# Hybrid decoder step (RG-LRU and mLSTM): other numbers of main matmuls between the side steps

## The chip, the cores and the metric

The kernel runs on one core of one Trainium2 chip. The metric is the device time of one execution in microseconds. Before the change the median of three timed runs is 949.22 us (947.42 to 950.13).

## The reference

One layer of a hybrid decoder step, on a prompt of 1024 positions (zero state) and on one new token for each of 8 sequences that already have a state. Both groups of heads read the same normalised input:

```
hn = rmsnorm(x, g_norm)
u = hn @ w_in                       # 1024 -> 7176
xa, za, q, k, v, o, zb, ui, uf = split(u)
yA = rglru(xa)                      # conv of 4 taps, two gates of 16 blocks 64x64, scan
yB = mlstm(q, k, v, ui, uf)         # 4 heads, DK = DV = 256, chunks of 128
yB = rmsnorm_head(sigmoid(o) * yB)
x = x + concat(yA * silu(za), yB * silu(zb)) @ w_out
y = rmsnorm(x, g_final)
```

RG-LRU: with `r`, `i` sigmoids of the block gates, `a = exp(-8 r softplus(-lam))`, and `h = a * h + sqrt(1 - a^2) * i * xc` is a scan over the positions. mLSTM carries a matrix `C` (256 x 256 for a head), a vector `n` and a running maximum `m`; one chunk uses the scores `q k^T` of its 128 positions with a decay mask, and the state for what lies before it. The outputs are both `y`, and for prompt and tokens the last `h`, the last three inputs of the conv, `C`, `n` and `m`. Everything is float32.

## The kernel before

**Main matmuls.** A float32 product is made of three fp32r matmuls: each operand is split into a high part (a cast on ScalarE, L70) and a low part (a subtraction on VectorE, L71), and `mm3` (L62 to L66) issues high x high, high x low and low x high. The input projection is cut into 14 units of two blocks of 256 columns, in the order `UNITS = v0v1 x0y0 q0k0 x1y1 q1k1 x2y2 v2v3 q2k2 x3y3 q3k3 o0o1 o2o3 z0z1 z2z3` (x is xa, y is za). A unit is computed by seven products of sums of blocks (`Q_P1` to `Q_P7`); `prep` builds the operand of one of them, two products ahead. `product(u, q)` runs one product in two halves and yields after each. The prediction calls one matmul of L64 to L66 a main.

**Side work.** Unit 0 runs at the start. For the other 13 units, after each half of a product, `pop_bg` takes steps from three queues: `bg` (two steps in unit 1 and in the last unit, else one), `rgq` (one), and `dcq` (one, at every second half of a product for units under 10, at every third from then on). A step issues a few instructions and so takes a place between main matmuls.

- `bg` holds first the generator `gates()`, one step a call (L563 to L666): the parameter rows are loaded and transposed (L588, PE), decays and exponentials are computed (L596 to L617), the rows of forget and input gates are transposed (L627, PE, into banks `ps_s` and `ps_qp`) and scanned (L632, L633, VectorE), four stacks of rows `stk` are written (L651 to L654), five empty steps follow (L655), and the stacks are transposed (L661, PE, one half of the chunks to `ps_s`, one to `ps_qp`). `rd_open` stands behind them: it opens the buffers of the gate weights and of the decode step.
- `rgq` holds the steps of RG-LRU for a block j of 128 channels and a half b of the positions, `rg_half`: `conv1`, `conv2`, `lows`, `gate_a` and `gate_b` (L786, PE: `ps_s<-xh` and `ps_tr<-xl`), `decay`, `scan`, `outs`. The prediction calls one such pair (j, b) a chunk of RG-LRU.
- `dcq` holds the decode steps of a head (`decode_steps`): `first`, then one `token(b)` for each of the 8 tokens. A token's state `Cb` is loaded on SyncE (L911), scaled on ScalarE (L932), updated on VectorE with the broadcast `vbc` (L905, L934), multiplied with q on PE (L953) and stored on GpSimd (L936).
- `dec_unit` computes the tokens' part of a unit's projection (L236) when its fifth product is prepared, and its turn (L244, a transpose, and L247, a reduction on VectorE) is run at one of the next pops. L236 and L244 use the PSUM bank `ps_tr`, as `gate_b` does. L261 and L262 build the operand of that product in place.

**The last unit and mLSTM.** When q, k and v of all heads are there and the queues are empty, `m_start` opens the mLSTM buffers and adds `m_first(n)` for the heads' first chunks: scores (L1126, L1128 on PE into `ps_s`), then the product with the state (`ps_qp<-Ch,qh`). In the last unit `wo_prep` loads the rows of the output projection (`oraw`, L1248 on SyncE), multiplies them with the tokens' merged values (L1270, PE, into `ps_tr`) and splits them (L1279, L1280, L71). Then the loop over the mLSTM chunks follows, with the output projection as its main matmuls.

**Order.** The program is written in the order of the loops, and a scheduler places each engine's instructions in a fixed queue by that order and by when it believes their operands to be ready. Each engine runs its queue in order. SyncE (SP) issues loads, GpSimd (POOL) issues stores; of the PSUM tiles, `ps_o` has three buffers, `ps_kv` two, and `ps_s`, `ps_qp` and `ps_tr` one each, which the prediction calls banks.

Of the kernel before, what the change touches and what calls it, by code (L numbers as in the profile page):

```python
# [20 lines left out]
NB = 8  # L21
# [28 lines left out]
def hymba_kernel(  # L50
# [17 lines left out]
    def split(hi, lo, src):  # L68

        A.copy(hi, src)  # L70
        V.tensor_tensor(lo, src, hi.bitcast(F32), op=ALU.subtract)  # L71
# [7 lines left out]
    def ps(tag, shape):  # L79
        return psp.tile(shape, F32, tag=tag, name=f"ps_{tag}", bufs=NBUF.get(tag, 1))  # L80
# [425 lines left out]
    kind, j = units[0][0]  # L506
# [61 lines left out]
    def gates():  # L568
# [48 lines left out]
        A.activation(dEM, dm, AF.Exp, scale=-1.0)  # L617
        stq(s_m, dm[0:1])
        yield

        rows = fp.tile([NH, 2, T], F32, tag="rows0", name="rows0")
        lfr, igr = rows[:, 0, :], rows[:, 1, :]
# [29 lines left out]
        A.copy(stk[32:36], br)  # L652
        V.tensor_tensor(c3(stk[64:68]), c3(br), aL.unsqueeze(2).to_broadcast([NH, NCH, L]), op=ALU.add)
        A.mul(stk[96:100], mr, -1.0)  # L654
        for _ in range(5):  # L655
            yield
        for half in range(2):
            pk = ps(("s", "qp")[half], [P, 4, P])
# [14 lines left out]
    bg, rgq, dcq = deque(), deque(), deque()  # L673
# [64 lines left out]
    def rg_gw(j):  # L738
        if j < KC:
            graw = fpr["graw"][j % 2]  # L740
            for n, src in enumerate((w_rgate, w_igate)):
                for s in LOHI:
                    ld(graw[s, :, n * 64:n * 64 + 64], src[0, 2 * j:2 * j + 2].rearrange("t c d -> c t d"))

    def rg_half(j, b):
        fp = fpr["p"]
        pc = lambda r, n=1: PT[:, j, r:r + n]
        st = {}

        n = 2 * j + b  # L750

        def conv1():
            rg_load(n, True)
            xs = st["xs"] = rst["x", n]
            rg_load(n + 1)
            if b == 0:
                rg_gw(j + 1)
                ghi = fp.tile([P, 2, P], F32R, tag="ghi", name="ghi")
                glo = fp.tile([P, 2, P], F32R, tag="glo", name="glo")
                split(ghi, glo, fpr["graw"][j % 2])  # L760
                rst["g", j] = ghi, glo
            st["xc"] = xc = fp.tile([P, HT], F32, tag="xc", name="xc")
            V.tensor_scalar(xc, xs[:, 3:3 + HT], pc(R_CW + 3), pc(R_CB), op0=ALU.mult, op1=ALU.add)
            for t in (2, 1):
                V.scalar_tensor_tensor(xc, xs[:, t:t + HT], pc(R_CW + t), xc, op0=ALU.mult, op1=ALU.add)

        def conv2():
            xs, xc = st["xs"], st["xc"]
            V.scalar_tensor_tensor(xc, xs[:, 0:HT], pc(R_CW), xc, op0=ALU.mult, op1=ALU.add)
            st["xx"] = [fp.tile([P, HT], F32R, tag=t, name=t) for t in ("xh", "xl")]  # L770
            for n, s in enumerate(LOHI):
                x = st["xx"][n]
                A.copy(x[s], xc[s])
            if b == 1:
                V.tensor_copy(OC[:, j, 1:4], xs[:, HT:HT + 3])

        def lows():
            for n, s in enumerate(LOHI):
                x = st["xx"][n]
                V.tensor_tensor(x[LOHI[1 - n]], st["xc"][s], x[s].bitcast(F32), op=ALU.subtract)  # L780

        def gate(n):

            pg = ps(("s", "tr")[n], [P, 512])
            for k, w in enumerate(rst["g", j]):
                TE.matmul(pg, w[:, n, :], st["xx"][n], start=k == 0, stop=k == 1)  # L786
            return pg

        def gate_a():
            rg_load(n + 1, True)  # L790
            pg = gate(0)
            st["rg"], st["ig"] = (fp.tile([P, HT], F32, tag=t, name=m) for m, t in (("rg", "rg"), ("ig", "xh")))
            gate_out(st["rg"], st["ig"], pg, j, 0)

        def gate_b():
            pg = gate(1)
            gate_out(st["rg"], st["ig"], pg, j, 1)
            st["na"] = fp.tile([P, HT], F32, tag="xl", name="na")
            A.activation(st["na"], st["rg"], AF.Tanh, scale=sp2[:, j:j + 1], bias=sp2[:, j:j + 1])
            A.activation(st["rg"], st["rg"], AF.Exp, scale=sp4n[:, j:j + 1], bias=sp4n[:, j:j + 1])  # L800
            V.scalar_tensor_tensor(st["ig"], st["ig"], 1.0, st["xc"], op0=ALU.add, op1=ALU.mult)

        def decay():
            rg, na = st["rg"], st["na"]
            V.scalar_tensor_tensor(na, rg, 1.0, na, op0=ALU.add, op1=ALU.mult)
            V.tensor_scalar(rg, na, -1.0, 1.0, op0=ALU.mult, op1=ALU.add)
            V.scalar_tensor_tensor(na, na, 2.0, na, op0=ALU.subtract, op1=ALU.mult)
            A.activation(na, na, AF.Sqrt, scale=-0.25)

        def scan():  # L810
            rg, ig, na = st["rg"], st["ig"], st["na"]
            V.tensor_tensor(ig, ig, na, op=ALU.mult)
            V.tensor_tensor_scan(na, rg, ig, 0.0 if b == 0 else OC[:, j, 0:1], op0=ALU.mult, op1=ALU.add)
            V.tensor_copy(OC[:, j, 0:1], na[:, HT - 1:HT])

        def outs():
            na, zs = st["na"], rst["z", n]
            V.scalar_tensor_tensor(na, na, 0.5, zs, op0=ALU.mult, op1=ALU.mult)
            mh, ml = sg([P, HT], "rmh", F32R), sg([P, HT], "rml", F32R)
            split(mh, ml, na)  # L820
            stq(d_rm[0, j, :, b * HT:(b + 1) * HT], mh.bitcast(F32))
            stq(d_rm[1, j, :, b * HT:(b + 1) * HT], ml.bitcast(F32))
        return [conv1, conv2, lows, gate_a, gate_b, decay, scan, outs]

    def rg_dec(j):

# [86 lines left out]
    def decode_steps(h):  # L913

        p2 = fpr["p"]
        qsel, qfirst, selq = fpr["qsel"], fpr["qfirst"], fpr["selq"]
        st = {}

        def first():
            st["kw"] = kw = p2.tile([P, 2, NB], F32, tag="kw", name="kw")  # L920
            V.tensor_tensor(kw, dk[:, 2 * h:2 * h + 2, :], dW[:, :, h].unsqueeze(1).to_broadcast([P, 2, NB]), op=ALU.mult)
            V.tensor_copy(qsel.rearrange("p k (m r) -> p k m r", r=9)[:, :, :, 0:5:4],
                          dq[:, 2 * h:2 * h + 2, :].rearrange("p k (m r) -> p k m r", r=2))
            V.tensor_copy(qfirst[:, :, :, 0], dq[:, 2 * h:2 * h + 2, 0:2])
            fetch_v(h, 0)

        def token(b):
            i = h * NB + b

            def f():  # L930
                vb_, C = ds_.pop(("v", i)), ds_["C", i]
                A.mul(C, C, dGI[:, b, h:h + 1])  # L932
                for kb in range(2):
                    V.scalar_tensor_tensor(C[:, kb, :], vb_, st["kw"][:, kb, b:b + 1], C[:, kb, :],  # L934
                                           op0=ALU.mult, op1=ALU.add)
                stq(s_C[0, b, h].rearrange("(kb p) v -> p kb v", p=P), C)  # L936
                if b + 1 < NB:
                    fetch_v(h, b + 1)
                if b % 2:
                    late.append(lambda: late.append(products))  # L940
                else:
                    fetch_C(i + 2)
                    fetch_C(i + 3)


            def products():
                if b == 1:
                    st["pq"] = ps("qp", [P, 512])
                pq = st["pq"]
                for g in range(4):  # L950
                    bb, kb = b - 1 + g // 2, g % 2
                    q, n = (qfirst[:, kb, bb, :], 32) if b == 1 else (qsel[:, kb, 4 * bb:4 * bb + 4], 4)
                    TE.matmul(pq[32 * g:32 * g + n, 0:256], q, ds_["C", h * NB + bb][:, kb, :], start=b == 1,  # L953
                              stop=b == NB - 1, skip_group_check=True)
                for bb in (b - 1, b):
                    del ds_["C", h * NB + bb]
                if b == NB - 1:
                    Z = sg([P, 256], "qC")
                    V.tensor_copy(Z, pq[:, 0:256])

                    def turn():
                        pt = pq[:, 256:272].rearrange("p (v b) -> p v b", v=2)
                        for vb in range(2):
                            TE.matmul(pt[:, vb, :], Z[:, vb * P:(vb + 1) * P], selq, start=True, stop=True)
                        V.tensor_copy(dqC[:, 2 * h:2 * h + 2, :], pt)
                    late.append(lambda: late.append(turn))
            return f
        return [first] + [token(b) for b in range(NB)]


    def bh(t):
# [454 lines left out]
    def preps(n):  # L1426
        while state["prep"] < min(n, len(seq)):
            prep(*seq[state["prep"]])
            state["prep"] += 1

    gg = gates()
    bg.extend([lambda: next(gg, None)] * 17 + [rd_open])
    last_u = len(units) - 1
    unit_of = {p: u for u, pair in enumerate(units) for p in pair}
    done_h = [max(unit_of[k, h] for k in "qkv") for h in range(NH)]
# [56 lines left out]
    for n in range(4, N):  # L1492
        c, h = n // 4, n % 4
# [84 lines left out]
```

## Time and profile before

| | before |
|---|---|
| timed runs, median (lowest to highest) | 949.22 us (947.42 to 950.13) |
| the profiled execution | 944.93 us |
| its span | 943.1 us |
| TensorE busy | 921.4 us |
| VectorE, ScalarE, GpSimd busy | 711.7, 587.2, 145.7 us |
| HBM read, written | 100.59, 51.65 MB |

The profile is one execution, with its own time. A row of a timeline gives the start in us, the length of the instruction (or of a run of like ones, with their count), the engine (PE is TensorE, DVE VectorE, ACT ScalarE, POOL GpSimd, SP SyncE), the line, the operation, what it writes and reads, its shape, and in brackets the idle time of the engine just before it with what ended it. Matmuls overlap, so the distance between two starts, and not the length, says what one costs. A row of waits gives what waited for what, with the sum, the count and the longest in us.

### The profile page before, as it was taken

How to read it: one execution, taken by the hardware profiler on the slowest of the kernel's cores; microseconds unless marked ns; L12 is line 12 of the kernel's file. 1: busy time of each engine (PE TensorE's matmuls, PEld its weight loads, DVE VectorE, ACT ScalarE, POOL GpSimd, SP SyncE). 2: the span in 40 equal slices, each digit the busy share in tenths (PEclk: the TensorE clock that was granted, in tenths of full speed). 3: DMA queues.
4: the chain of work that ended last, by engine and by line, in shares of the span. 5: the costliest groups of instructions: out<-in, count | busy, mean ns of one | idle time of the engine just before them, and what ended most of it. 6: DMA issues, size and time to landing. Idle time of an engine off the chain costs nothing. (4 is left out here: it accounts for less than half of the span.)

```text
span 943.1 us, 15351 instructions
## 1 busy us (share of the span) xinstructions
PE 921.4 (98%) x5350; PEld 761.0 (81%) x5350; DVE 711.7 (75%) x1465; ACT 587.2 (62%) x1052; POOL 145.7 (15%) x259
## 2 busy tenths in 40 slices
PE   9999999999999999999999999999899999999997
PEld 7797767777787987787789898876578888888886
DVE  6784898889798878888797867687657676676764
ACT  7563457778677757677578774467537466555532
POOL 1111112112112122111122221010201000000020
PEclk9999999999999999999999999999999999999999
DMA  5521347356746464545557362426953564464461
GB/s 174 187 82 45 134 132 276 107 181 203 243 145 207 157 207 165 176 140 189 193 180 248 131 209 87 157 88 229 343 159 111 162 187 122 142 187 140 122 103 46
DMA packets 131384, 153.19 MB, mean 162 GB/s; under 512 B 15817, under 2 KB 110057, under 8 KB 131299
## 3 DMA queue, kind: packets, MB, share of 16 engines
q1 hardware_dynamic: 113578, 96.34, 34.0%
q0 software_dynamic: 17728, 55.87, 16.5%
q8 instruction: 42, 0.69, 0.3%
q14 instruction: 36, 0.29, 0.1%
HBM read 100.59 MB, written 51.65 MB: 161 GB/s over the span
## 5 line engine op out<-in xcount | busy, mean ns | idle before, releaser
L71 DVE TENSOR_TENSOR wl<-raw,wh 128x1024 fp32r<-128x1024 f32 x91 | 110.9, 1219 | 27.2 <-ACT wh L70 17.2
L70 ACT CAST wh<-raw 128x1024 fp32r<-128x1024 f32 x91 | 95.4, 1048 | 54.9 <-PE ps_o L65 23.3
L64 PE MATMUL ps_kv<-cb_hi,wh 128*128 128x512 f32 x320 | 127.8, 399 | 0.6 <-ACT s L319 0.6
L66 PE MATMUL ps_kv<-cb_hi,wl 128*128 128x512 f32 x320 | 125.3, 392 | 0.0
L65 PE MATMUL ps_kv<-cb_lo,wh 128*128 128x512 f32 x320 | 125.2, 391 | 0.0
L64 PE MATMUL ps_o<-cb_hi,wh 128*128 128x512 f32 x240 | 95.1, 396 | 0.0
L66 PE MATMUL ps_o<-cb_hi,wl 128*128 128x512 f32 x240 | 94.0, 392 | 0.0
L65 PE MATMUL ps_o<-cb_lo,wh 128*128 128x512 f32 x240 | 93.6, 390 | 0.0
L64 PEld LDWEIGHTS ps_kv<-cb_hi,wh 128*128 128x128 f32 x320 | 60.1, 188 | 22.1 <-issue 4.2
L66 PEld LDWEIGHTS ps_kv<-cb_hi,wl 128*128 128x128 f32 x320 | 60.1, 188 | 13.9 <-issue 0.8
L65 PEld LDWEIGHTS ps_kv<-cb_lo,wh 128*128 128x128 f32 x320 | 60.2, 188 | 12.6 <-issue 0.8
L64 PE MATMUL ps_kv<-wh,cb_hi 128*128 128x256 f32 x192 | 55.4, 288 | 0.0
L64 PEld LDWEIGHTS ps_o<-cb_hi,wh 128*128 128x128 f32 x240 | 45.1, 188 | 11.5 <-issue 2.5
L65 PE MATMUL ps_kv<-wl,cb_hi 128*128 128x256 f32 x192 | 54.3, 283 | 0.0
L66 PE MATMUL ps_kv<-wh,cb_lo 128*128 128x256 f32 x192 | 54.3, 283 | 0.0
L64 PE MATMUL ps_o<-wo,rh 128*128 128x512 f32 (+1 forms) x136 | 53.8, 396 | 0.0
L65 PEld LDWEIGHTS ps_o<-cb_lo,wh 128*128 128x128 f32 x240 | 45.1, 188 | 10.0 <-issue 0.8
L66 PEld LDWEIGHTS ps_o<-cb_hi,wl 128*128 128x128 f32 x240 | 45.1, 188 | 9.8
L66 PE MATMUL ps_o<-wo,ml 128*128 128x512 f32 (+1 forms) x136 | 52.1, 383 | 0.7 <-DVE ml L71 0.7
L64 PE MATMUL ps_o<-wo,mh 128*128 128x512 f32 (+1 forms) x136 | 52.8, 388 | 0.0
L66 PE MATMUL ps_o<-wo,rl 128*128 128x512 f32 (+1 forms) x136 | 51.8, 381 | 0.3 <-DMA rl<-d_rm 0.3
L65 PE MATMUL ps_o<-wo,rh 128*128 128x512 f32 (+1 forms) x136 | 51.6, 379 | 0.0
(481 smaller groups left out, 2530.2 us busy)
## 6 DMA issues: line engine op xcount, KB each, us to landing
raw<-in_w_in_dram SPq DMA_DIRECT2D x55, 512.0 KB
Cb<-in_state_mlstm_C_dram SPq DMA_DIRECT2D x32, 256.0 KB
out_dram<-Cb POOLq DMA_DIRECT2D x32, 256.0 KB, 4.6
qk<-d_qk SPq DMA_DIRECT2D x32, 256.0 KB
oraw<-in_w_out_dram SPq DMA_DIRECT2D x16, 512.0 KB
d_qk<-s POOLq DMA_DIRECT2D x24, 256.0 KB, 3.9
d_x<-s POOLq DMA_DIRECT2D x16, 256.0 KB, 2.6
zsr<-d_y SPq DMA_DIRECT2D x16, 256.0 KB
```

Of the source, the lines that this page charges most:

```text
L64: TE.matmul(out, ah, bh, start=first, stop=False, skip_group_check=True)
L65: TE.matmul(out, ah, bl, start=False, stop=False, skip_group_check=True)
L66: TE.matmul(out, al, bh, start=False, stop=last, skip_group_check=True)
L70: A.copy(hi, src)
L71: V.tensor_tensor(lo, src, hi.bitcast(F32), op=ALU.subtract)
```

## The change

Five edits, all of them empty steps: in the generator of the gates one more yield ahead of the transposes of the rows, and seven empty steps for five ahead of the transposes of the stacks; the queue calls the generator 18 times for 17; for the first halves (b = 0) of the blocks j = 0 and 1, RG-LRU's queue has an empty step ahead of `gate_a`; head 0's decode has one between `first` and the first token.

```diff
@@ -617,6 +617,7 @@
         A.activation(dEM, dm, AF.Exp, scale=-1.0)
         stq(s_m, dm[0:1])
         yield
+        yield
 
         rows = fp.tile([NH, 2, T], F32, tag="rows0", name="rows0")
...
@@ -652,7 +653,7 @@
         V.tensor_tensor(c3(stk[64:68]), c3(br), aL.unsqueeze(2).to_broadcast([NH, NCH, L]), op=ALU.add)
         A.mul(stk[96:100], mr, -1.0)
-        for _ in range(5):
+        for _ in range(7):
             yield
         for half in range(2):
             pk = ps(("s", "qp")[half], [P, 4, P])
...
@@ -820,7 +821,8 @@
             stq(d_rm[1, j, :, b * HT:(b + 1) * HT], ml.bitcast(F32))
-        return [conv1, conv2, lows, gate_a, gate_b, decay, scan, outs]
+        wait = [lambda: None] if j < 2 and b == 0 else []
+        return [conv1, conv2, lows] + wait + [gate_a, gate_b, decay, scan, outs]
@@ -965,7 +967,7 @@
             return f
-        return [first] + [token(b) for b in range(NB)]
+        return [first] + [lambda: None] * (h == 0) + [token(b) for b in range(NB)]
@@ -1429,7 +1431,7 @@
     gg = gates()
-    bg.extend([lambda: next(gg, None)] * 17 + [rd_open])
+    bg.extend([lambda: next(gg, None)] * 18 + [rd_open])
```

## The prediction

> **What bounds the kernel now.** I read the busy shares and the chain of waits first, then TensorE's waits, then the stretches around the largest ones.
>
> ```profile
> span 943.1 us, 15351 instructions
> PE 921.4 (98%) x5350; PEld 761.0 (81%) x5350; DVE 711.7 (75%) x1465; ACT 587.2 (62%) x1052; POOL 145.7 (15%) x259
> PE 18%; DVE 3%; DMA 2%; issue 1%; ACT 0%; SPq 0%; DVEq 0%; ACTq 0%
> PE ps_tr L1270 <- DMA oraw<-in_w_out_dram: 2.8, 3, 2.0
> PE ps_s L661 <- DVE stk L653: 1.7, 1, 1.7
> PE ps_s L786 <- DVE xh L780: 1.6, 2, 1.3
> PE ps_kv L64 <- ACT s L319: 0.6, 1, 0.6
> PE ps_s L627 <- DVE gx L599: 0.3, 1, 0.3
> ```
>
> TensorE (PE) is busy for 921.4 of 943.1 us, and it leads the chain. A change of order can win only what PE loses in waits, about 22 us in all, plus clock. The waits are in us: total, times, longest. The steps of the gates that the change moves are L627, L661 and L786; their waits add up to 0.3 + 1.7 + 1.6 us. The largest single wait stands elsewhere, at the start of the mLSTM stage, and it has a price beyond itself:
>
> ```profile
> 120.00:140.00 20.00, 18.32 (x90) 14.58 (x87) 19.85 (x38) 8.65 (x19) 3.64 (x9) 1.00 0.48 139
> 680.01 1.93 PE L1270 MATMUL ps_tr<-oraw,mBd 128*32 128x512 f32 x8 [2.01 <-DMA oraw<-in_w_out_dram]
> 680.00:682.00 2.00, 1.99 (x9) 0.33 (x9) 0.77 (x1) 1.15 (x1) 0.59 (x2) 0.50 1.17 305
> 682.00:684.00 2.00, 2.00 (x8) 1.81 (x9) 0.88 (x3) 1.09 (x3) 0.55 (x1) 0.65 1.19 299
> 684.00:686.00 2.00, 2.00 (x11) 1.62 (x10) 0.59 (x2) 0.26 (x1) 0.00 (x0) 1.00 1.07 339
> ```
>
> The columns of the windows: length, busy PE, weight loads, DVE, ACT, POOL, granted clock, DMA share, GB/s. After the 2.01 us gap the clock is 0.50 in one window and 0.65 in the next. That loses 2 x 0.50 + 2 x 0.35 = 1.70 us, so the gap costs 3.7 us. The gap of 1.7 us at L661 lies in the first of these windows, whose clock is 1.00.
>
> **The change part by part.** The built instruction lists of the two kernels hold the same instructions; only their order differs. I call the wide products of L64 to L66 "mains"; one takes 0.23 us (140.72 to 140.95 below). Positions are counted in mains ahead of an instruction:
>
> ```
> gates rows, L627 (ps_qp)        +12 and +4
> gates, L588, L627 (ps_s), L661  no change
> first gate product, chunk (0,0) no change (629)
> chunk (0,1) ps_s, ps_tr         +12, +17 (720 -> 737)
> chunk (1,0) ps_s                +23 (805 -> 828)
> later chunks                    +18 to +49
> first decode product, L953      +36 (828 -> 864)
> first score products, L1126     +48 (2688 -> 2736)
> score products of chunk 4       -24 (3096 -> 3072)
> from main 3168 on (709 us)      no difference
> ```
>
> *The gates (an extra yield, 7 for 5 empty ones, 18 generator steps).* Their waits stand at L661 and L786:
>
> ```profile
> 125.15 1.22 DVE L653 TENSOR_TENSOR stk<-rows,gsm 4x1024 f32<-4x1024 f32 x1
> 126.51 0.63 PE L661 MATMUL ps_s<-idF,stk 128*128 128x128 f32 x4 [1.68 <-DVE stk L653]
> 141.31 0.89 DVE L934 SCALAR_TENSOR_TENSOR Cb<-vbc,kw,Cb 128x256 f32<-128x256 f32 x2 [1.18 <-DMA vbc<-d_dv]
> 143.07 0.47 PE L786 MATMUL ps_s<-xh,ghi 128*128 128x512 f32 x1 [1.28 <-DVE xh L780]
> ```
>
> Seven mains' time, 1.6 us, would cover the 1.68, but in the built order no main moves ahead of L661, although the source asks for two more steps: the scheduler places the transposes where it believes them ready. The same holds for the first L786, which stands behind xh, itself behind the L934 that waited 1.18 us for a DMA; DVE, POOL and SP keep their order up to about 143 us. I take 0 for all three. If the scheduler's placing were otherwise, at most 0.3 + 1.68 + 1.28 = 3.3 us could be won. The ps_qp transposes that do move had no wait to lose.
>
> *The empty step ahead of chunk (1,0)'s gates, and the shift of all chunks.* Two waits lose their place:
>
> ```profile
> 188.76 0.47 PE L786 MATMUL ps_s<-xh,ghi 128*128 128x512 f32 x1 [0.36 <-DVE xh L780]
> 370.93 0.62 ACT L70 CAST rmh<-na 128x512 fp32r<-128x512 f32 x1 [1.99 <-DVE na L818]
> 372.58 0.50 PE L64 MATMUL ps_kv<-cb_hi,wh 128*128 128x512 f32 x1 [0.58 <-ACT s L319]
> 140.72 0.39 PE L65 MATMUL ps_kv<-cb_lo,wh 128*128 128x512 f32 x1
> 140.95 0.39 PE L66 MATMUL ps_kv<-cb_hi,wl 128*128 128x512 f32 x1
> ```
>
> At 188.76 us, 23 more mains (5.3 us) stand ahead, so 0.36 us is gone. At 372.58 us PE waits for a copy, L319, that stands in ScalarE's queue behind the cast of a chunk's rmh, which itself came late (1.99 us) from DVE. That chunk moves by 24 mains, 5.5 us, so the two no longer meet and 0.58 us goes too. Together -0.94 at best, and 0 if what comes in their place is as late; I take -0.9.
>
> One meeting gets worse. Chunk (0,1)'s ps_tr product now stands five mains behind the turn L244, whose bank it reuses, so it must wait for L247 to empty that bank. In DVE's new order L261, L262 and a weight split (L71) stand between:
>
> ```profile
> 167.59 1.92 PE L236 MATMUL ps_tr<-raw,hnd 128*32 128x512 f32 x16
> 170.70 0.60 PE L244 MATMUL ps_tr<-idF,Z 128*128 128x128 f32 x4
> 171.06 0.48 PE L64 MATMUL ps_kv<-cb_hi,wh 128*128 128x512 f32 x1
> 163.07 0.69 DVE L780 TENSOR_TENSOR xl<-xc,xl 64x512 fp32r<-64x512 f32 x1
> 169.09 1.22 DVE L261 TENSOR_TENSOR raw<-raw 128x1024 f32<-128x1024 f32 x1
> 170.83 1.22 DVE L262 TENSOR_TENSOR raw<-raw,raw 128x1024 f32<-128x1024 f32 x1
> 171.96 0.35 DVE L247 TENSOR_REDUCE dxz<-ps_tr 128x16 f32<-128x64 f32 x2
> 172.08 1.05 ACT L70 CAST wh<-raw 128x1024 fp32r<-128x1024 f32 x1 [0.59 <-DVE raw L262]
> 173.22 1.22 DVE L71 TENSOR_TENSOR wl<-raw,wh 128x1024 fp32r<-128x1024 f32 x1
> ```
>
> Half of L236 frees the operand of L261. From there DVE and ACT need L261 1.22, L262 1.22, the cast 1.05, the split 1.22, L247 0.35: 5.1 us. PE meanwhile has the other half of L236 (0.96), 12 mains (2.8), L244 (0.36, 170.70 to the next at 171.06) and 5 mains (1.15): 5.3 us. So the two meet, and hand-overs between the engines decide: I take a new wait of 0.2 us, between 0 and 2.5, which is three DVE operations (3.66) less five mains (1.15), if DVE comes to L261 only at L244's end. Against that end: xl, the last work ahead of L261 in the new order, ended at 163.8 us, some 2 us before half of L236 would end there (L236 moves up by seven mains, 1.6 us, and half of it is 0.96).
>
> *The empty step in head 0's decode.* Its first products, L953, had no wait; token updates L934 move between the gate chunks, and the DMAs of vbc behind them. L934 waited 1.18 us once. The window below has DVE busy for 17.55 of its 20 us, so a stall can be made good, and no PE wait in 144 to 636 us comes out negative when I add up what moves past it, beside the one above; I take 0, with the 1.2 us as the loss if a stall reaches PE, and no gain, since L953 waited for nothing.
>
> ```profile
> 140.00:160.00 20.00, 18.72 (x83) 15.11 (x83) 17.55 (x30) 14.54 (x21) 3.84 (x6) 1.00 0.79 265
> ```
>
> *The start of the mLSTM stage (636 to 700 us).* Here the shift of 24 to 48 mains pays or costs.
>
> ```profile
> 666.78 4.58 SPq L1248 DMA_DIRECT2D oraw<-in_w_out_dram  x4
> 667.24 1.07 PE L1270 MATMUL ps_tr<-oraw,mAd 128*32 128x512 f32 x8 [0.49 <-DMA oraw<-in_w_out_dram]
> 690.46 0.60 PE L1126 MATMUL ps_s<-qk 128*128 128x128 f32 x4
> 690.90 0.38 PE L1128 MATMUL ps_s<-idF,qk 128*128 128x128 f32 x2
> 691.04 0.48 PE L64 MATMUL ps_o<-wo,rh 128*128 128x512 f32 x1
> 688.82 0.28 PE L65 MATMUL ps_tr<-vl,ph 128*128 128x258 f32 x1
> 688.94 0.28 PE L66 MATMUL ps_tr<-vh,pl 128*128 128x258 f32 x1
> ```
>
> Chunk 4's score work now stands ahead of the last oraw wait instead of behind it: half of L1126 x4 (0.44 / 2 = 0.22), L1128 x2 (0.14), two products with the state of the size of those at 688.82 (0.12 each, 0.24), two mains (0.46): 1.06 us that PE does while it waits. The last oraw, on which it waits, is issued in the same place, at the end of the four issues from 666.78 us, behind a DVE split that doesn't move; the two before it go out 1 to 2 us earlier, since the mains that release them come earlier. So I leave its landing at 680.0 us; the wait shrinks from 2.01 to about 0.95 us. The 0.49 us ahead of it can only shift into it. Gain 1.0 us, between 0 (the landing moves as much) and 2.0 (the whole wait).
>
> The clock follows from the length of the gap: 1.68 us was borne, 2.01 was not, so about 1 us should be. That returns 1.7 us, or 0.
>
> The Trainium skill, "TensorE: Matmul & The Clock Gate", Part 1, says that the clock falls after an idle window of about 3.4 us. By that rule a 2.01 us gap would not lower it; the trace differs, with 0.50 right behind such a gap. By the page, the sum would keep no 1.7 us for the clock, which is rival B's time.
>
> ```profile
> 688.24 0.35 DVE L1106 SCALAR_TENSOR_TENSOR W<-W,be_t,maskT 128x128 f32<-128x128 f32 x1 [3.65 <-DMA W<-d_alpha]
> ```
>
> Behind it, SP issues the z load after the next qk load, and W no longer waits for pf. DVE waited 3.65 us for W while PE ran its mains (689 us); so 0, and at most 3.65 to either side if that cover were gone. From 709 us on, the order is the same and shifts along.
>
> **Sum.** 0 (gates) - 0.9 + 0.2 - 1.0 - 1.7 = -3.4 us. The profiled execution took 944.9 us, with a span of 943.1; it lies 4.3 below the median of the three timed runs (947.4 to 950.1). I subtract from the median: 949.2 - 3.4 = 945.8 us.
>
> **The rivals.**
>
> *A, as summed: 945.8.* Bounds without the rivals: -0.9 - 2.0 - 1.7 = -4.6 (944.6), to +0.2 - 0.3 - 1.7 = -1.8 (947.4) with the gap only just under the 1.68 that the clock bore. Chance 0.50.
>
> *B, the half clock stays: 947.5.* Either a gap of this length isn't what lowers it (the low stretch itself lasted 1.70 / 0.50 = 3.4 us, and a gap as long as that stands nowhere near), or the last oraw lands later, since DMA is already at a share of 1.07 to 1.19 there and the earlier loads crowd it. The single case in the trace doesn't fix the threshold; against it speaks that after 1.68 us nothing fell. 949.2 - 3.4 + 1.7. Chance 0.20.
>
> *C, nothing remains: 949.2.* The waits that the change is about stay where they are, and the small gains are eaten by stalls of L934 (1.2 us) and a landing that follows (1.0). Chance 0.10.
>
> *D, slower: the meeting at L247.* If DVE comes late to L261, PE waits 2.5 us instead of 0.2, and a gap of that size halves the clock as the one at 680 us did: +2.3 + 1.7 = +4.0 on A, 949.8; with B's clock as well 951.5. It decides from a wait of about 2 us; for it speaks DVE's load (17.55 of 20 us), against it the 2 us between xl and L261. Chance 0.20.
>
> **How the numbers follow.** About 0.3% (2.8 us) can be told from no change, so faster means under 946.4, slower over 952.0. A lies under with 0.75 of its chance, B with 0.25, giving 0.43, and I say 0.45. The scatter of the runs (1.8 below and 0.9 above the median) puts half of D and a third of B and C over: 0.10 + 0.07 + 0.03 = 0.20. That leaves 0.35 for the same. The range runs from A's lower bound less the scatter, 944.6 - 1.8 = 942.8, to D's upper 951.5; A's own is 944.6 to 947.4.
>
> **What would show it.** Waits of 1.7 us at L661 and 1.3 us at the first L786 as before (in the changed kernel the lines lie one or two further down). No wait of 0.36 at chunk (1,0), none of 0.58 before 373 us. A wait of 0 to 0.5 us at chunk (0,1)'s ps_tr product, near 171 us. One of about 1 us for the last oraw near 679 us, and a granted clock of 1.00 behind it. I am wrong if the L661 wait goes, if an idle stretch of 2 us or more appears between 144 and 200 us, or if the clock is 0.5 after the oraw wait. An execution that differs from 945.8 by more than that is due to a place behind 700 us that I took as shifting along.

## The result, and the profile after

| | before | after |
|---|---|---|
| median of 11 timed runs each | 947.42 us | 952.28 us |
| ratio, with its 95% interval | 1 | 1.0054 (1.0035 to 1.0072) |
| profiled execution, its span | 944.93, 943.1 us | 952.18, 950.4 us |
| TensorE busy | 921.4 us | 922.7 us |

The change makes the kernel slower by about 5.1 us (0.54% of 947.4; the medians lie 4.9 us apart); 945.8 us was predicted. That forecast took 3.4 us off a median of three runs, 949.22 us, which lies 1.8 us above the median of the eleven; taken off 947.42 it would be 944.0 us. The profile of before was one of that kernel's faster executions, so the two spans lie further apart (7.3 us) than the medians.

The waits of TensorE (PE) in the changed kernel, in us as total, times, longest; its lines stand one or two further down:

```profile
PE ps_tr L1272 <- DMA oraw<-in_w_out_dram: 2.9, 4, 1.2
PE ps_kv L64 <- ACT s L319: 2.9, 2, 1.6
PE ps_tr L1321 <- DVE hh L1191: 2.3, 2, 2.0
PE ps_s L872 <- DVE ORow L873: 2.1, 1, 2.1
PE ps_s L662 <- DVE stk L654: 1.7, 1, 1.7
PE ps_s L787 <- DVE xh L781: 1.6, 1, 1.6
```

And where the large ones stand, in the timeline of PE in the same kernel:

```profile
126.91 0.63 PE L662 MATMUL ps_s<-idF,stk 128*128 128x128 f32 x4 [1.68 <-DVE stk L654]
241.58 0.50 PE L64 MATMUL ps_kv<-cb_hi,wh 128*128 128x512 f32 x1 [1.58 <-ACT s L319]
510.77 0.39 PE L64 MATMUL ps_kv<-wh,cb_hi 128*128 128x256 f32 x1 [1.32 <-ACT s L319]
573.94 0.61 PE L872 MATMUL ps_s<-idF,OC 128*20 128x128 f32 x4 [2.07 <-DVE ORow L873]
685.11 1.06 PE L1272 MATMUL ps_tr<-oraw,mBd 128*32 128x512 f32 x8 [0.42 <-DMA oraw<-in_w_out_dram]
689.83 1.07 PE L1272 MATMUL ps_tr<-oraw,mBd 128*32 128x512 f32 x8 [1.16 <-DMA oraw<-in_w_out_dram]
708.62 1.04 PE L1321 MATMUL ps_tr<-zd,sel 128*32 128x512 f32 x2 [2.04 <-DVE hh L1191]
```

The gates' wait of 1.68 us stands where it stood. The oraw gap of 2.01 us is now 1.16, and the clock stays up behind it. But three waits are new, of 1.58, 1.32 and 2.07 us, and the longest of them, at 573.94 us, brings the low clock with it. The windows of that stretch (length, PE, weight loads, DVE, ACT, POOL, granted clock, DMA share, GB/s):

```profile
574.00:576.00 2.00, 2.00 (x15) 1.95 (x16) 1.34 (x3) 0.83 (x2) 0.00 (x0) 0.79 0.28 72
576.00:578.00 2.00, 2.00 (x11) 2.00 (x11) 0.00 (x0) 0.35 (x1) 0.72 (x2) 0.50 0.00 0
578.00:580.00 2.00, 2.00 (x17) 2.00 (x16) 0.00 (x0) 0.25 (x1) 2.00 (x4) 0.86 0.43 139
```

That loses 2 x (0.21 + 0.50 + 0.14) = 1.7 us, so by this trace the stop at L872 costs 3.8 us. Why it stops is in VectorE's queue, shown here for the changed kernel:

```profile
565.75 0.23 DVE L859 TENSOR_TENSOR OC<-dgr 128x64 f32<-128x64 f32 x1
568.92 0.62 DVE L1108 SCALAR_TENSOR_TENSOR W<-W,be_t,maskT 128x128 f32<-128x128 f32 x2 [2.94 <-DMA W<-d_alpha]
571.48 0.35 DVE L1108 SCALAR_TENSOR_TENSOR W<-W,be_t,maskT 128x128 f32<-128x128 f32 x1 [0.95 <-DMA W<-d_alpha]
571.74 1.22 DVE L71 TENSOR_TENSOR wl<-raw,wh 128x1024 fp32r<-128x1024 f32 x1
573.22 0.67 DVE L873 COPY ORow<-ps_s 20x512 f32<-20x512 f32 x1
574.67 0.67 DVE L873 COPY ORow<-ps_s 20x512 f32<-20x512 f32 x1
```

L872 transposes the rows of RG-LRU in two halves through the one ps_s; the second half waits until L873 has copied the first away. L873 stands behind the decay masks W of mLSTM, and these stand and wait for their loads, 2.94 and 0.95 us. Before the change the same queue ran through:

```profile
554.84 0.61 DVE L1106 SCALAR_TENSOR_TENSOR W<-W,be_t,maskT 128x128 f32<-128x128 f32 x2
560.48 0.68 DVE L871 COPY ORow<-ps_s 20x512 f32<-20x512 f32 x1 [0.63 <-PE ps_kv L65]
```

The issues on SyncE say why the loads are late. Before, the first two W go out at 547.64 us, and the next weights (two loads of 512 KB) at 559.28; after, the weights go out at 560.46 and W directly behind them. SyncE's queue stands at these weights for 11.8 us, until VectorE frees their buffer, with W behind them. Before the change VectorE comes to the masks 7.2 us after W went out and doesn't wait; in the changed kernel it is ready for them 4.5 us after, and W is there after 7.4. First the changed kernel, then the one before:

```profile
560.46 0.92 SPq L223 DMA_DIRECT2D raw<-in_w_in_dram  x2
561.48 1.51 SPq L1086 DMA_DIRECT2D W<-d_alpha  x2
564.26 0.48 SPq L1086 DMA_DIRECT2D W<-d_alpha  x1
```

```profile
547.64 0.81 SPq L1084 DMA_DIRECT2D W<-d_alpha  x2
559.28 0.95 SPq L223 DMA_DIRECT2D raw<-in_w_in_dram  x2
```

The waits for L319 are a matter of ScalarE's queue. In the 5 us ahead of 241.58 us it has no idle time at all in the changed kernel:

```profile
236.42 1.28 ACT L737 ACT_TABLE_LOAD   x1
237.72 1.09 ACT L737 ACTIVATE dgr<-ps_s,hb 64x8 f32<-64x8 f32 x4
238.83 1.05 ACT L70 CAST wh<-raw 128x1024 fp32r<-128x1024 f32 x1
239.78 0.61 ACT L70 CAST rmh<-na 128x512 fp32r<-128x512 f32 x1
240.31 0.61 ACT L774 CAST xh<-xc 64x512 fp32r<-64x512 f32 x1
240.94 0.59 ACT L319 COPY s<-ps_kv 128x512 f32<-128x512 f32 x1
```

The steps of two chunks and of the tokens' gates (dgr, with a table load of 1.28 us) have come to stand ahead of the copy that frees PE's output. Ahead of 510.77 us the same kinds of steps stand there, with two short waits for VectorE (0.44 and 0.53 us).

### The profile page after: what moved, and what is told of

It is laid out like the page before. It is cut to its first block, busy times and chain, and to the rows that moved or that the text cites. A ratio compares the mean times of both kernels' runs of the same rounds, so it can differ in the third digit from the quotient of the medians.

```text
span 950.4 us, 15354 instructions
## 1 busy us (share of the span) xinstructions
PE 922.7 (97%) x5350; PEld 762.0 (80%) x5350; DVE 711.7 (75%) x1465; ACT 586.6 (62%) x1052; POOL 145.6 (15%) x259
## 4 chain that ended last, share of the span: by engine, by line
PE 73%; DVE 10%; DMA 8%; ACT 4%; issue 3%; SPq 1%; POOL 0%; DVEq 0%; ACTq 0%; POOLq 0%
PE ps_o L66 12%; PE ps_o L64 12%; PE ps_o L65 12%; PE ps_kv L64 9%; PE ps_kv L65 8%; PE ps_kv L66 8%; DMA W<-d_alpha 3%; DMA oraw<-in_w_out_dram 2%; PE ps_tr L236 2%; PE ps_s L1128 1%; DMA Cb<-in_state_mlstm_C_dram 1%; DVE wl L71 1%; DMA x<-in_x_prompt_dram 1%; PE ps_qp L955 1%; PE ps_s L787 1%
## 5 line engine op out<-in xcount | busy, mean ns | idle before, releaser
L65 PEld LDWEIGHTS ps_kv<-cb_lo,wh 128*128 128x128 f32 x320 | 60.1, 188 | 11.8
```

The lines of the kernel that those rows point to most:

```text
L65: TE.matmul(out, ah, bl, start=False, stop=False, skip_group_check=True)
```

## The experiments

The built order says beforehand what each edit moves; positions are mains ahead of the instruction.

```
                          before  gates_only  rg_only  dec_only  tail2  after
stk transposes               569         569      569       569    569    569
chunk (1,0), ps_s            805         805      828       805    805    828
first decode products        828         828      828       864    828    864
RG-LRU rows, two halves  2616/2647  2616/2647  2664/2695  2616/2647  2616/2647  2664/2695
first scores of mLSTM       2688        2688     2736      2688   2736   2736
```

So all shifts of the chunks, of the rows and of mLSTM come from the empty step ahead of `gate_a`, and those of the decode products from the one in head 0's decode. The runs follow, with the ratio to the kernel before in shared rounds.

**rg_only** keeps that step alone:

```diff
+        wait = [lambda: None] if j < 2 and b == 0 else []
+        return [conv1, conv2, lows] + wait + [gate_a, gate_b, decay, scan, outs]
```

> Only the empty step ahead of gate_a (j < 2, b = 0). Theory: this edit alone moves the chunks of RG-LRU (12 to 48 mains later), the last transposes of its rows and the start of mLSTM, and it carries the whole loss: ratio to the kernel before 1.004 to 1.007, with the wait of about 2 us at the second transposes of the RG-LRU rows (572 us), a low clock behind it, and a wait of over 1 us for ScalarE's L319. Rival (the empty decode step is what collides, since the waits for L319 stand right behind decode products): ratio 1.000 to 1.002 and no wait for L319.

Measured: 1.0038 (1.0022 to 1.0055), and the stop at the rows is there:

```profile
572.44 0.70 PE L871 MATMUL ps_s<-idF,OC 128*20 128x128 f32 x4 [1.91 <-DVE ORow L872]
```

Two waits for L319 stand beside it, the longest 1.10 us, and the clock is low for 3.4 us from 572.81 us on. The places are those of the theory; the ratio lies just under the 1.004 it named, and whether this step carries the whole loss can't be told from it. The profile is the longest of its 11 executions, 954.87 us.

**gates_only** keeps the three edits of the gates:

```diff
+        yield
...
-        for _ in range(5):
+        for _ in range(7):
...
-    bg.extend([lambda: next(gg, None)] * 17 + [rd_open])
+    bg.extend([lambda: next(gg, None)] * 18 + [rd_open])
```

> Only the gates' part (an extra yield, seven empty steps for five, 18 calls for 17). Theory: two transposes move and nothing else, so the ratio is 0.998 to 1.002 and the wait ahead of the transposes of stk stays at 1.5 to 1.8 us. Rival (the two moved transposes delay the row scans): the wait ahead of the stk transposes grows to over 2.2 us and the clock falls behind it, ratio over 1.002.

Measured: 1.0003 (0.9988 to 1.0018). The timeline of PE in it:

```profile
126.56 0.63 PE L662 MATMUL ps_s<-idF,stk 128*128 128x128 f32 x4 [1.67 <-DVE stk L654]
700.59 1.92 PE L1320 MATMUL ps_tr<-zd,sel 128*32 128x512 f32 x2 [2.36 <-DVE hh L1190]
```

The gates' part does nothing that can be measured. The second row is of use too: with the order of before, the wait ahead of the final product of the tokens is 2.36 us here and was 0.83 in the profile of before; VectorE waits 3.56 us for W ahead of it here, and 2.03 there. So the 2.04 us at 708.62 us after the change lies within the scatter of W's landing and isn't counted as its cost.

**dec_only** keeps the empty step in head 0's decode:

```diff
-        return [first] + [token(b) for b in range(NB)]
+        return [first] + [lambda: None] * (h == 0) + [token(b) for b in range(NB)]
```

> Only the empty step in head 0's decode. Theory: the first decode products move by 36 mains and the rest of the order hardly, so the ratio is 0.998 to 1.002 with no new wait over 0.6 us. Rival (this edit makes the waits for ScalarE's L319): a wait of 1 to 2 us behind a decode product near 240 or 510 us and a ratio of 1.002 to 1.004.

Measured: 1.0043 (1.0024 to 1.0061), against the theory, and the wait isn't the rival's either. First PE, then ScalarE in this kernel:

```profile
264.82 0.66 PE L244 MATMUL ps_tr<-idF,Z 128*128 128x128 f32 x4 [1.62 <-ACT Z L239]
265.41 0.61 PE L953 MATMUL ps_qp<-Cb,qsel 128*4 128x256 f32 x6
```

```profile
261.05 0.62 ACT L773 CAST xh<-xc 64x512 fp32r<-64x512 f32 x1 [3.22 <-DVE na L813]
262.16 1.05 ACT L70 CAST wh<-raw 128x1024 fp32r<-128x1024 f32 x1 [0.49 <-DVE raw L262]
263.67 0.62 ACT L70 CAST rmh<-na 128x512 fp32r<-128x512 f32 x1 [0.46 <-DVE na L818]
264.19 0.58 ACT L239 COPY Z<-ps_tr 128x512 f32<-128x512 f32 x1
```

A unit's turn, L244, has come into the middle of a run of token products. It waits for a copy that stands in ScalarE's queue behind three casts, each late for an input of its own, and the rest of the run is held behind it. Before, the copy ended at 262.1 us and the turn came at 262.86, without a wait.

**tail2** leaves RG-LRU and decode where they were and moves only the start of mLSTM:

```diff
-            rgq.extend([rg_final, lambda: None, rg_rows])
+            rgq.extend([rg_final, lambda: None, rg_rows] + [lambda: None] * 2)
```

> The kernel before with two empty steps behind the RG-LRU rows, so that only the start of mLSTM moves to where the changed kernel has it (2736 mains) and the RG-LRU and decode steps stay. Theory: the gain at the last oraw load remains (a wait of 0.8 to 1.5 us for 2.0, clock 1.00 behind it) and the losses go, so ratio 0.996 to 0.999. Rival (the later start of mLSTM is itself the loss, through its later W loads): ratio 1.002 or more, with DVE waits for W ahead of PE waits between 560 and 720 us.

Measured: 0.9992 (0.9978 to 1.0006), short of the theory's 0.996 to 0.999. The gap at the last oraw load and the window behind it:

```profile
681.77 1.07 PE L1270 MATMUL ps_tr<-oraw,mBd 128*32 128x512 f32 x8 [1.42 <-DMA oraw<-in_w_out_dram]
```

```profile
682.00:684.00 2.00, 2.00 (x13) 1.05 (x6) 1.01 (x1) 1.49 (x2) 1.12 (x2) 1.00 1.00 281
```

So the later score products alone don't slow the kernel; the mechanism of the gain is there, but what it is worth, 0.08%, can't be told from nothing. The rival, later loads of W, isn't tested here: SyncE issues the first two at 547.71 us, as before the change (547.64). rg_bank below has them late.

**dec_again** is dec_only once more:

> The kernel with only the empty step in head 0's decode once more, for a second profile, since the first one fell on its fastest execution (947.5 us, median 951.8). Theory: a typical execution shows two or more extra waits between 195 and 560 us, where head 0's tokens meet other work on ScalarE and VectorE, summing to 3 us or more over the kernel before. Rival: up to 640 us it differs by less than 1.5 us and the loss stands at the oraw loads (a gap over 2 us and a low clock behind it).

Measured: 956.33 us in this one run, a wait of 1.74 us at the same place, 2.34 us at an oraw load and 2.81 ahead of the tokens' last product. It is slower than all 12 executions of dec_only, so it isn't the typical one that was sought. Neither side came as worded: between 195 and 560 us there is one new wait, not two or more, and 1.6 us more waiting than before, not 3; but across that turn the mains fall back by 4.8 us against before (from 2.9 to 7.6 us later), made of 1.74 us of waiting, 1.7 us from the low clock of the windows below, and 1.3 us that is left for the moved and broken run of products. The first 2.9 us arise ahead of 60 us, long before this step.

```profile
268.00:270.00 2.00, 2.00 (x13) 1.19 (x12) 2.00 (x6) 1.83 (x4) 0.54 (x1) 0.82 0.85 304
270.00:272.00 2.00, 2.00 (x6) 1.54 (x6) 2.00 (x2) 0.38 (x1) 0.00 (x0) 0.50 0.92 279
272.00:274.00 2.00, 2.00 (x9) 1.60 (x8) 0.76 (x2) 1.41 (x2) 0.00 (x0) 0.83 0.09 31
```

**dec_hold** takes that meeting away and leaves the decode step as it is. hold(i, k) makes instruction i follow group k of three mains (counted from 0) in the issue order, by an edge that costs no semaphore; what stands behind # is an explanation:

```diff
+                r = TE.transpose(pt[:, m, :], Z[:, m * P:(m + 1) * P], idF)
+                if u == 5:
+                    hold(r, 363)    # queued behind main 1092
```

> The kernel with only the empty decode step, and an order edge that holds the turn (L244) of unit 5's decode products 12 mains later (1092 for 1080), behind head 0's token products and out of their middle. Theory: in the kernel with the empty step alone PE waited 1.62 and 1.74 us there for ScalarE's copy L239, which stands behind a chunk's casts, and with the broken run of products and the low clock that can follow it is most of that kernel's loss; so no wait there, and the ratio falls from 1.0043 to 1.000 to 1.002. Rival (the loss comes from other meetings): wait gone, ratio still 1.003 or more.

Measured: 1.0018 (1.0001 to 1.0036), for 1.0043 without the edge; the difference is 0.25%, give or take 0.25. The traces say more: from main 1056 to main 1104 the mains fall back against before by 0.7 us here, by 3.1 in dec_only and by 4.8 in dec_again. In its timeline the eight products run in one piece and the turn (L250 here) doesn't wait:

```profile
264.27 0.61 PE L961 MATMUL ps_qp<-Cb,qsel 128*4 128x256 f32 x8
267.68 0.60 PE L250 MATMUL ps_tr<-idF,Z 128*128 128x128 f32 x4
```

**all_bank** is the changed kernel with another PSUM tile for the second half of the rows; **rg_bank** is rg_only with the same edit:

```diff
-            po = ps("s", [20, 4, P])
+            po = ps(("s", "qp")[half], [20, 4, P])
```

> The changed kernel with the second half of the RG-LRU rows transposed into another PSUM tile (ps_qp for ps_s), so that it doesn't wait for VectorE's copy of the first half, which stands behind W. Theory: the 2.07 us wait and the low clock behind it go (1.7 us), so the ratio to the kernel before falls from 1.0054 to 1.000 to 1.003. Rival (the time comes back at the oraw loads, whose landing decides): no wait at the rows, but ratio still 1.004 or more and the oraw waits longer by 2 us or more.

> The kernel with only the empty step ahead of gate_a, and the second half of the RG-LRU rows transposed into ps_qp. Theory: the 1.9 us wait at the rows and its low clock go, the waits for ScalarE's L319 (0.3 to 1.1 us each) stay: ratio 1.000 to 1.002, for 1.0038 without the other tile. Rival (the later chunks cost as much elsewhere): 1.003 or more.

Measured: all_bank 1.0029 (1.0013 to 1.0045), rg_bank 1.0005 (0.9991 to 1.0020); no wait at the rows in either. That stop is worth 0.25% of the changed kernel (1.0054 less 1.0029, 2.4 us, give or take 2.3) and 0.33% of rg_only (3.1 us, give or take 2.1). In the traces the stop stands alone: between mains 2640 and 2720 the changed kernel falls back by 3.7 us against all_bank, and rg_only by 3.6 against rg_bank, as the reading of 3.8 had it. With it gone, rg_only can't be told from the kernel before, while two waits for L319 (0.56 and 1.03 us) stay; with the decode step as well the one near 241 us is 1.57 us. That in rg_bank they and the gains at 188 and 372 us about cancel fits the ratio, but isn't shown. In all_bank 0.29% is left; its trace has three waits for L319 (0.41, 1.57 and 1.24 us) and none at L244.

**hold_both** does what the words of the change say, later gate steps, by edges that the scheduler can't pass over (the lines stand in two places); **hold_tail** adds the two steps of tail2, and **hold_tail_2** repeats it:

```diff
+                hold(TE.transpose(pk[:, q, :], stk[:, c * P:(c + 1) * P], idF), 192)    # 579 for 569
...
+                if (j, b) == (0, 0):
+                    hold(g, 215)    # 648 for 629
```

> The kernel before with what the change names done in fact: an order edge holds the stk transposes 10 mains later (579 for 569) and chunk (0,0)'s gate products 19 mains later (648 for 629). Theory: the waits of 1.68 and 1.3 us go and VectorE makes good the rest in its idle time after 144 us, ratio 0.996 to 0.999. Rival (VectorE is the bound there, so the waits only move on): new waits of 2 us or more in sum between 145 and 200 us, ratio 0.999 to 1.001.

> As hold_both, and two empty steps behind the RG-LRU rows, which put the start of mLSTM where the changed kernel has it. Theory: both gains add, ratio 0.994 to 0.998. Rival (what is won before 200 us is lost at the oraw loads, which land when DMA is done): ratio 0.999 to 1.000.

> hold_tail once more (stk transposes 10 and chunk (0,0)'s gate products 19 mains later by order edges, start of mLSTM two steps later): ratio 0.9965 to 0.999 again, if its gain is real; 0.999 to 1.001 if it was scatter.

Measured: hold_both 0.9991 (0.9978 to 1.0005), hold_tail 0.9978 (0.9965 to 0.9990) and again 0.9977 (0.9960 to 0.9993). The waits of L661 and of the first gate product are gone, but the first comes back 10 mains later, at the transposes of the decode rows. First PE in hold_both, then ScalarE in hold_tail:

```profile
131.38 0.60 PE L892 MATMUL ps_s<-idF,dqk 128*8 128x128 f32 x4 [1.90 <-ACT em_t L672]
```

```profile
128.32 1.05 ACT L76 CAST wh<-raw 128x1024 fp32r<-128x1024 f32 x1 [2.64 <-DVE raw L268]
130.75 0.18 ACT L670 ACTIVATE gi_t<-ps_s 128x16 f32<-128x16 f32 x1 [1.38 <-DVE be_t L669]
131.08 0.23 ACT L672 ACTIVATE em_t<-ps_qp 128x16 f32<-128x16 f32 x1
```

em_t stands directly behind a step that waited 1.38 us for VectorE, so this wait hangs on VectorE as the one at L661 did. The rival has the ratio and the moving on, but not the place: between 145 and 200 us only 0.87 us of waiting stands in hold_both, not 2.

**hold_rows** holds those transposes too, 10 mains:

> As hold_tail, and the transposes of the decode rows of v (which took over the wait, 1.9 us at 131 us, for ScalarE's em_t) held 10 mains later too (594 for 584). Theory: that wait goes as well and up to 1.9 us more is won, ratio 0.995 to 0.998. Rival (the loads of vbc, which hang on these rows, come 2 us later and VectorE stands longer for them, so PE waits behind it near 150 us): ratio as hold_tail or worse, with a wait of 1.5 us or more between 145 and 160 us.

Measured: 0.9975 (0.9960 to 0.9990). That wait goes, and one of 1.44 us appears at a gate product at 163 us; the gain is no larger than hold_tail's. hold_tail and hold_rows are about 2 us faster than the kernel before and, by the two ratios, about 0.8% faster than the changed one.

## Why the prediction was wrong

*The gates: 0.* Right: gates_only gives 1.0003 (0.9988 to 1.0018), with the wait of 1.67 us in place.

*The two waits that lose their place: -0.9.* Right: neither 0.36 us near 189 us nor 0.58 us near 373 us is among the waits after. But L319 now meets other steps at 241.58 and 510.77 us (1.58 and 1.32 us), the case the prediction allowed for when it said 0 "if what comes in their place is as late", so by the trace nothing of the 0.9 is left.

*The meeting at L247: +0.2, and rival D from it.* No wait over 0.15 us stands there after. D had the right sign for a reason that didn't occur, so that its 949.8 us lies nearest to the measured time is luck. (By the prediction's own figures half of L236 would end 3.2 us behind xl, 167.59 - 1.6 + 0.96 - 163.8, not some 2 us, which speaks more strongly against D.)

*The oraw wait: -1.0, and the clock: -1.7.* The clock behind it stays at 1.00, as forecast. The wait of 2.01 us became 0.42 and 1.16, but the other waits of the stage grew: 0.34, 0.49, 0.33 and 2.01 before (3.2 us) stand against 0.81, 0.55, 0.51, 0.42 and 1.16 after (3.5). What PE did ahead of one wait it waited at another. The later score products alone gave 0.9992: about 0.8 us (0.6 lost to 2.1 won) in place of 2.7, a term mis-sized. Part of that is that wait and clock differ from execution to execution: in gates_only, with the order of before at this place, the longest wait for oraw is 1.09 us and the clock stays at 1.00 behind it. So the low stretch is no fixed 1.7 us in a median. The mean granted clock is 0.9975 over the 12 runs of tail2 and 0.9964 over the 34 of before in the same rounds, a difference of about 1 us.

*The step that failed* is the sentence "no PE wait in 144 to 636 us comes out negative when I add up what moves past it". It summed durations against the slack in the profile of before, and a queue isn't a sum of durations: its head stands still for inputs that the sum doesn't hold. At 573.94 us these were DMA loads (2.94 and 0.95 us, ahead of a copy of 0.67), which had landed in time because they were issued ahead of 1 MB of weights and not behind them. The price was 3.7 us in the trace and 2.4 to 3.1 us in the ratios, where the sum had 0. At L244 they were three casts that each waited for VectorE. I named the stall of a token step (1.2 us) as the price of the decode step; the runs put about 2.4 us on one meeting of it with a unit's turn (2.3 us by the traces of dec_only and dec_hold). And I took the 3.65 us that DVE waited for W at 688 us as harmless, and didn't ask what stands behind W where the queue has other work, 110 us earlier.

What stays open: the waits for L319 are read from the trace and weren't taken away by themselves, so that the 0.29% left in all_bank is theirs is not shown. Nor is the 0.18% left in dec_hold explained. The two edits cost 0.38 and 0.43% alone and 0.54% together; the L244 wait is missing in the profile after and the L319 wait near 241 us is longer (1.58 us for 0.75 in rg_only), so they may displace each other, but a sum for that is not shown.

## What to carry to other kernels

An empty step in a list that is popped at a fixed rate doesn't move one instruction, it moves every later step of that list against all other lists, and each new meeting on an in-order queue can cost a microsecond or two (up to 2.1 us of waiting here, at times with 1.7 us of clock). Where a scheduler places by readiness, an empty step may move nothing at all: look at the built order first, and use an explicit edge for the one instruction that is meant. When a move is costed, read for each engine what the instructions ahead in its new queue wait for, the DMA loads above all, not only how long they run.

## What the runs showed of the hardware

The granted clock changes on a fixed grid. In the records of before it rises at 14.40 us, falls at 680.00, rises at 683.42 and falls at 939.42 us; the distances are 665.60, 3.41 and 256.00 us, which are 195, 1 and 75 times 3.4133 us, and in all 14 profiles the changes lie on such a grid, whose phase differs from run to run. The table adds up PE's idle time in each of these windows, without the last 10 us of each run, where the kernel ends:

```
idle time of PE in one window of 3.41 us    windows    followed by a window at half clock
1.51 to 1.72 us                             23         0
1.74 to 1.90 us                              7         3
1.91 to 2.54 us                              7         7
```

So in these traces somewhat over half a window of idle time halves the clock for the next 3.41 us, and a gap that a boundary splits counts in two parts: 2.34 us at 663 us in dec_again was split into 1.18 and 1.16, and the clock stayed. At L244 both gaps lay whole in one window: 1.62 us in dec_only cost no clock, and 1.74 us in dec_again, in the band where it went either way, cost another 1.7 us. The prediction's rule, that 1.68 us is borne and 2.01 not, had the right limit and lacked the phase. The Trainium skill, "TensorE: Matmul & The Clock Gate", Part 1, gives a free-running window of 3413 ns, which the traces confirm. The advice in its section "Why this matters for your kernels", to have no idle gaps of over about 3 us, is too lenient here, since 1.91 us and more in one window was enough each time.
